# Hybrid decoder trunk: seven products for eight in the second matrix of each MLP's fourth quarter

## The chip, the cores and the metric

The kernel runs on one core of one Trainium2 chip. The metric is the device time of one execution in microseconds (us). The core has a matrix engine (TensorE, PE in the profile; PEld is its weight load), a vector engine (VectorE, DVE), a scalar engine with function tables (ScalarE, ACT), GpSimd (POOL) and SyncE (SP), which issues the transfers. Matrix products are accumulated in PSUM (8 banks of 512 float32 columns); all else lies in SBUF. Each engine works through its own queue in order, and waits on semaphores for the others.

## The reference

Two layers over 528 positions (16 learned meta tokens and 512 inputs) of width 1024, in float32:

```
layer 0: h = h + mixer(rms_norm(h))          sliding-window attention and Mamba-2, then w_out
         h = h + square(relu(rms_norm(h) @ w_up[0])) @ w_down[0]
layer 1: h = h + conformer(rms_norm(h))      pw1, sigmoid gate, causal convolution of 31 taps,
                                             layer norm, SiLU, pw2
         h = h + square(relu(rms_norm(h) @ w_up[1])) @ w_down[1]
out = h without the meta positions
```

`w_up` is 1024 x 4096 and `w_down` 4096 x 1024 in each layer; `pw1` is 1024 x 2048, `pw2` 1024 x 1024.

## The kernel before

**Layout.** Activations are held transposed: 128 channels on the partitions, positions along the row. The 528 positions are cut into stream A (272 positions, 256 after the meta tokens are dropped) and stream B (256). A product takes a 128x128 tile of weights as the loaded operand and one stream's columns as the moving one.

**Precision.** A float32 product is made from three in the type `float32r`. Each operand is split in a high part, a rounded copy, and a low part, the rest: hi x hi, hi x lo and lo x hi are accumulated in one bank (`products`, L456). Splitting a piece of weights costs a cast on ScalarE (`th_cast`, L410, tile `wh`) and a subtraction on VectorE or GpSimd (`th_low`, L423, tile `wl`). Activations are split likewise (`ah` and `al`, `nh` and `nl`).

**Stages.** An MLP goes in four quarters q of 1024 hidden channels. "up" makes eight hidden tiles: `ev_up` (L1325) does relu with the norm's factor `rb` (VectorE), the square (ScalarE), the copy `ah` (ScalarE) and the rest `al` (VectorE). "dn" multiplies them with the matching quarter of `w_down` into eight output tiles, and `ev_dn` (L1340) adds each to `h`. In the profile `up03A` is layer 0, quarter 3, stream A. With a positive `lead`, `dense` (L468) begins that many output tiles together, does the first `cut` of their inner tiles, and only then the rest: this covers the wait for the last inputs. After w_out the order is: layer 0 A q2, q3 (A q0, q1 are done earlier); pw1 of A, `pw1(0)`; layer 0 B q0 to q3; `pw1(1)` of B; `pw2(0)`; layer 1 A q0 to q3; `pw2(1)`; layer 1 B q0 to q3. The last quarter of a stream ends with `prep` (L1225), which makes the next norm's inputs, or with `fin` (L1604), which writes the output. In layer 1 both streams have 256 columns.

**The convolution.** `th_conv` (L1484) runs on VectorE in the background, 31 taps for each of 8 channel tiles of a stream, in PSUM, once pw1's evacuation has written the gated tiles `U`. `th_ln` (L1528) then makes the layer norm and SiLU and writes the split inputs of pw2, `KHr[0]` and `KLr[0]` for A and `AH[1]` for B. Ahead of `pw2(0)` and of `pw2(1)` the main thread waits for this thread (`pause("ln")`).

**Weights.** `expect` lists the pieces of all weights in the order of use; `th_load` brings them through SyncE into a pool of wide buffers (8 tiles, 512 KB) or narrow ones (4 tiles, 256 KB), with 3 and 4 buffers each for raw, high and low parts.

**What sets the order.** All instructions are written down by a list scheduler (`Sched`, L66) when the kernel is built. Threads offer one operation at a time; `step` (L177) takes the one that can start first by modelled times, ties going to the lower priority number (evacuations 0.5, casts, layer norm 1, convolution 3, products 5). An operation may have two ways, VectorE or GpSimd; `emit` (L121) takes the one that ends first. In this model VectorE operations with two inputs in SBUF and GpSimd operations exclude each other ("port"). For the low parts `bias` is added to VectorE's end: 600 ns, 3000 from pw1(0) on, 0 from pw2(1) on. On the chip only the order within each queue and the choice of engine remain.

## Time and profile before

| | |
|---|---|
| median of 3 runs | 1237.41 us (1237.12 to 1237.72) |
| profiled execution | 1237.84 us, of which the span from first to last instruction is 1236.1 us |
| mean granted TensorE clock | 0.994 |
| TensorE busy | 1219.7 us, 9939 matrix instructions |
| VectorE, ScalarE, GpSimd busy | 861.5, 683.4, 549.5 us |
| loaded from HBM | 190.62 MB |

A time of a stretch is written as from:to in microseconds from the span's start. In a group of instructions `out<-in` names what is written and read, then partitions x elements, the count, the busy time and the mean of one, and last the engine's idle time before them with what ended it. Matrix instructions overlap in the pipeline, so a mean of 285 ns doesn't mean that one starts every 285 ns.

### The profile page before, as it was taken

The page shows a single profiled execution, that of the slowest core. Times are in us where ns is not written, and L with a number is a line of the kernel's source. Part 1 is how long each engine was busy: PE and PEld are TensorE (multiplying, and loading weights), DVE is VectorE, ACT ScalarE, POOL GpSimd, SP SyncE. Part 2 cuts the span into 40 slices and gives each one's busy share as a digit, 9 for nine tenths or more (in the row PEclk, how much of TensorE's full clock was granted, in tenths as well). Part 3 has the DMA queues.
Part 4 walks back from the last instruction along what each step waited for, and adds up shares of the span by engine and source line. Part 5 has one row for each costly group of instructions (what it writes and reads, how often), then busy time and mean ns, then how long its engine had stood idle before and what let it go on. Part 6 is the DMA issues. An engine that isn't in the chain of part 4 may idle for free.

```text
span 1236.1 us, 25626 instructions
## 1 busy us (share of the span) xinstructions
PE 1219.7 (99%) x9939; PEld 1176.1 (95%) x9939; DVE 861.5 (70%) x1915; ACT 683.4 (55%) x1277; POOL 549.5 (44%) x339
## 2 busy tenths in 40 slices
PE   8999998999999999999999999999999999999998
PEld 7999887799898999999999999999999999999998
DVE  6745685787785675658989965589898626766664
ACT  6654235677475663654544568556345645644542
POOL 0112331354541111148888878888888781000000
PEclk8999999999999999999999999999999999999999
DMA  6323112344344765546555555565555566566562
GB/s 191 105 81 86 44 44 56 104 141 144 114 142 135 245 198 176 172 135 199 183 184 181 185 166 180 187 192 175 181 186 183 176 194 202 188 179 196 177 196 91
DMA packets 79961, 194.38 MB, mean 157 GB/s; under 512 B 8912, under 2 KB 16608, under 8 KB 79840
## 3 DMA queue, kind: packets, MB, share of 16 engines
q1 hardware_dynamic: 79840, 192.75, 50.2%
q8 instruction: 78, 1.28, 0.4%
q14 instruction: 43, 0.35, 0.1%
HBM read 190.62 MB, written 2.10 MB: 156 GB/s over the span
## 4 chain that ended last, share of the span: by engine, by line
PE 92%; DVE 3%; ACT 3%; issue 1%; DMA 1%; SPq 0%; DVEq 0%; ACTq 0%
PE in L308 11%; PE pw L308 9%; PE out L308 5%; PE dn00A L308 2%; PE up00A L308 2%; PE up01A L308 2%; PE up03A L308 2%; PE dn02A L308 2%; PE dn12A L308 2%; PE up03B L308 2%; PE dn13B L308 2%; PE dn12B L308 2%; PE dn11B L308 2%; PE dn10B L308 2%; PE dn11A L308 2%; PE dn03B L308 2%
## 5 line engine op out<-in xcount | busy, mean ns | idle before, releaser
L256 POOL TENSOR_TENSOR wl<-wr,wh 128x1024 fp32r<-128x1024 f32 (+1 forms) x292 | 519.2, 1798 | 432.1 <-ACT wh L280 315.3
L280 ACT CAST wh<-wr 128x512 fp32r<-128x512 f32 (+1 forms) x494 | 384.6, 801 | 287.7 <-PE in L308 35.1
L254 DVE TENSOR_TENSOR wl<-wr,wh 128x512 fp32r<-128x512 f32 (+1 forms) x202 | 189.3, 949 | 90.0 <-ACT wh L280 87.1
L261 DVE SCALAR_TENSOR_TENSOR conv<-U,vec,conv 128x256 f32<-128x256 f32 x464 | 211.3, 484 | 5.2
L308 PE MATMUL in<-xh,wh 128*128 128x272 f32 (+1 forms) x384 | 103.6, 296 | 1.4 <-ACT wh L280 1.2
L308 PE MATMUL in<-xl,wh 128*128 128x272 f32 (+1 forms) x384 | 100.8, 289 | 1.1 <-DVE xl L261 1.1
L308 PE MATMUL pw<-nh,wh 128*128 128x256 f32 (+1 forms) x320 | 80.3, 285 | 0.0
L308 PE MATMUL pw<-nl,wh 128*128 128x256 f32 (+1 forms) x320 | 80.1, 284 | 0.0
L308 PEld LDWEIGHTS in<-xh,wh 128*128 128x128 f32 x384 | 73.3, 191 | 6.9 <-issue 3.2
L308 PEld LDWEIGHTS in<-xl,wh 128*128 128x128 f32 x384 | 73.3, 191 | 2.3 <-DVE xl L261 2.0
L308 PE MATMUL in<-xh,wl 128*128 128x272 f32 (+1 forms) x384 | 66.9, 291 | 0.0
L308 PEld LDWEIGHTS pw<-nl,wh 128*128 128x128 f32 x320 | 60.3, 189 | 0.0
L308 PEld LDWEIGHTS pw<-nh,wh 128*128 128x128 f32 x320 | 60.2, 188 | 0.1
L308 PEld LDWEIGHTS in<-xh,wl 128*128 128x128 f32 x384 | 55.0, 192 | 1.6 <-issue 0.9
L308 PE MATMUL pw<-nh,wl 128*128 128x256 f32 (+1 forms) x320 | 48.4, 284 | 0.0
L276 ACT ACT_TABLE_LOAD x30 | 38.5, 1283 | 9.0 <-DMA hin<-in_h 4.6
L308 PEld LDWEIGHTS pw<-nh,wl 128*128 128x128 f32 x320 | 42.8, 188 | 0.0
L308 PE MATMUL out<-xh,wh 128*128 128x272 f32 (+1 forms) x128 | 33.0, 288 | 0.2 <-ACT acc L276 0.2
L308 PE MATMUL out<-xl,wh 128*128 128x272 f32 (+1 forms) x128 | 32.6, 285 | 0.0
L254 DVE TENSOR_TENSOR pw<-pw,rb 128x272 f32<-128x272 f32 (+1 forms) x32 | 14.1, 440 | 24.9 <-PE pw L308 24.9
L308 PEld LDWEIGHTS out<-xh,wh 128*128 128x128 f32 x128 | 24.1, 188 | 1.4 <-issue 0.8
L308 PEld LDWEIGHTS out<-xl,wh 128*128 128x128 f32 x128 | 24.1, 188 | 0.0
(597 smaller groups left out, 3642.5 us busy)
## 6 DMA issues: line engine op xcount, KB each, us to landing
wr<-in_w_up SPq DMA_DIRECT2D x84, 512.0 KB, 3.7
wr<-in_w_dn SPq DMA_DIRECT2D x84, 512.0 KB, 4.0
wr<-in_w_up SPq DMA_DIRECT2D x88, 256.0 KB, 4.3
wr<-in_w_dn SPq DMA_DIRECT2D x88, 256.0 KB, 4.3
wr<-in_w_p SPq DMA_DIRECT2D x36, 512.0 KB, 3.9
wr<-in_w_in SPq DMA_DIRECT2D x48, 256.0 KB, 2.9
wr<-in_w_out SPq DMA_DIRECT2D x36, 256.0 KB, 2.8
wr<-in_w_p SPq DMA_DIRECT2D x24, 256.0 KB, 5.2
```

Source lines behind the costliest of these rows:

```text
L254: ways = [("V", 1.04 * n + 145, lambda: nc.vector.tensor_tensor(o, a, b, op=op), sb(a) and sb(b))]
L256: ways.append(("G", 2.17 * n + 170, lambda: nc.gpsimd.tensor_tensor(o, a, b, op=op), True))
L261: lambda: nc.vector.scalar_tensor_tensor(o, a, s, b, op0=op0, op1=op1), sb(a) and sb(b))],
L276: return Op([("A", ns, lambda: nc.scalar.activation(o, a, f, **kw), False)], aps(o, accum), aps(a, scale, bias), table=TABLE.get(f, 0))
L280: return Op([("A", 0.836 * cols(o) + 192, lambda: nc.scalar.copy(o, a), False)], [o], [a])
L308: nc.tensor.matmul(o, lhsT=l, rhs=r, start=st, stop=sp)
```

## The change

The dn matrix of quarter 3 is done for both streams at once, in both layers. Two rows of weight tiles and two halves of the inner tiles make a 2x2 block matrix W, the halves of the hidden channels and the two streams a 2x2 block matrix (X for A, Y for B). Strassen's scheme (in Winograd's form) makes the product with seven block products in place of eight. It needs four sums of weight blocks per pair of rows (`th_sum`, tile `ws`, on VectorE or GpSimd) and four sums of activation blocks (`sums_of`), each split in high and low parts, and sums of the results: `ev` in `seven` and `add_part` or `fin_part`, which add to `h` in two steps. The sums of activations lie in the room of `U` and `Y`, the convolution's tiles, which are now taken for the time of the convolutions only.

For this, both streams' up of quarter 3 go together, tile by tile, in the order 0, 4, 1, 5, 2, 6, 3, 7, and the order of the stages changes. Layer 0: A's q2 is cut in two halves of four hidden tiles, one before and one after the joint q3; B's q0 to q2 follow pw1(0) as before. Layer 1: A q0 to q2 before pw2(1), B q0 to q2 after it, the joint q3 last. `late=False` lets B's q0 in layer 0 apply the norm's factor in up rather than in dn.

Two more edits act on the whole kernel. In `step`, while a thread of priority up to 0.5 offers an operation for VectorE that excludes GpSimd, other threads' GpSimd operations that would end after its start are held off. `row_norm` keeps one PSUM bank for both of its steps instead of two in turn.

```diff
         for th in self.threads:
             op = th[3]
             if op is None:
                 continue
...
+            t = min(self.start(op, w)[0] for w in ways)
             t = max(t, op.dep + op.late)
-            p = th[1]
-            p = p() if callable(p) else p
+            p = rank(th)
...
+    def expect_seven(pairs):
+
+
+        for one, two in pairs:
+            i = len(plan)
+            half = lambda j, x: (j, 4 * x)
+            plan.extend((("wp", one, 8, None), ("wp", two, 8, "raw"),
+                         ("wm", (ALU.add, half(i + 1, 0), half(i + 1, 1)), 4, "sum"),
+                         ("wm", (ALU.subtract, half(i, 0), half(i + 1, 0)), 4, "sum"),
+                         ("wm", (ALU.subtract, half(i + 2, 0), half(i, 0)), 4, "sum"),
+                         ("wm", (ALU.subtract, half(i, 1), half(i + 4, 0)), 4, "sum"),
+                         ("wm", half(i + 1, 1), 4, "half")))
+            uses.extend((4, 4, 2, 1, 2, 1, 1))
...
+            if plan[i][3] == "sum":
+                op, (a, x), (b, y) = plan[i][1]
+                yield lambda: a in raws and b in raws
+                t = yield take(wm, [128, 4, 128], F32, "raw", 4, "ws")
+                o = TT(t, raws[a][:, x:x + 4], raws[b][:, y:y + 4], op, True)
+                o.ways[0] += (bias[0] / 2,)
+                yield o
+                raws[i] = t
+                used_raw(a, b)
...
-        yield BM(*((p[:, i:i + 1], a[:, blk(c)[0] - b0:blk(c)[0] - b0 + 128], ones[:, 0:1], True, True)
+        yield BM(*((p[:, 496 + i:497 + i], a[:, blk(c)[0] - b0:blk(c)[0] - b0 + 128], ones[:, 0:1], True, True)
...
-        yield TS(v, p[:, :nb], 1.0 / D, eps, ALU.mult, ALU.add)
-        drop(p)
+        yield TS(v, p[:, 496:496 + nb], 1.0 / D, eps, ALU.mult, ALU.add)
...
-        p = yield bank("bg", "st" + key)
...
+            if last:
+                raw[s, j] = yield take(pool7[0], [128, 272], F32, "sq", 8)
+                r = raw[s, j][:, :w]
+                yield ACT(r, u, AF.Square)
+                drop(p)
+                sums.add((s, j))
+                if s == 0 or j >= 4:
+                    yield CP(ah[:, j, :w], r)
+                    yield TT(al[:, j, :w], r, ah[:, j, :w].bitcast(F32), ALU.subtract)
+                    up[i].add(j)
+                return
...
+        if last:
+            summed = [set() for _ in range(4)]
+            flat.clear()
+            for t, x in (("U", TAPS - 1 + T), ("Y", T)):
+                flat.append((yield take(pool7[0], [128, 8 * x], F32R, t, 1)))
+            for k in range(4):
+                spawn(sums_of(k, streams[0][4], sums, raw, up, summed), 1, name + "sum")
+        yield from dense(name, nts, 8, [t[1:5] for t in streams], ev_up, lead, cut, [has(t[6]) for t in streams])
+        name = name.replace("up", "dn")
+        if last:
+            yield from seven(name, streams, up, summed, last)
+        else:
+            yield from dense(name, range(8), m, [(t[7], t[8], 0, t[4]) for t in streams], ev_dn,
+                             dlead, dcut, [(lambda k, u=u: k in u) for u in up])
...
+    SEVEN = (0, 4, 1, 5, 2, 6, 3, 7)
...
+    def sums_of(k, w, there, raw, up, summed):
+        yield lambda: {(0, k), (1, k)} <= there
+        x1, y1 = raw[0, k], raw[1, k]
+        yield lambda: k in up[0]
+        yield TT(x1[:, :256], y1[:, :256], x1[:, :256], ALU.subtract, True)
+        yield lambda: (1, k + 4) in there
+        y2 = raw[1, k + 4]
+        yield TT(y1[:, :256], y2[:, :256], y1[:, :256], ALU.subtract, True)
+        yield lambda: k + 4 in up[1]
+        yield TT(y2[:, :256], y2[:, :256], x1[:, :256], ALU.subtract, True)
+        if w > 256:
+            yield VCP(y2[:, 256:w], x1[:, 256:w])
+        yield lambda: k + 4 in up[0]
+        x2 = raw[0, k + 4]
+        yield TT(x2[:, :w], y2[:, :w], x2[:, :w], ALU.subtract, True)
+        for i, t in ((1, x1), (3, y1), (2, y2), (4, x2)):
+            n = w if i in (2, 4) else 256
+            hi, lo = slot(i, 0, k, n), slot(i, 1, k, n)
+            yield CP(hi, t[:, :n])
+            yield TT(lo, t[:, :n], hi.bitcast(F32), ALU.subtract, True)
+            drop(t)
+            summed[i - 1].add(k)
+
+    def seven(name, streams, up, summed, part):
...
+        def sbank():
+            t = pmm(name)()
+            return t if t is not None else bank("at", name)()
+
+        def product(p, hi, lo, x, first, last_, ks=range(4)):
+            xh_, xl_, when, n = ops[x]
+            for k in ks:
+                yield lambda: when(k)
+                yield MM([(p[:, :n], hi[:, k], xh_(k), first and k == 0, False),
+                          (p[:, :n], hi[:, k], xl_(k), False, False)])
+            for k in ks:
+                yield MM([(p[:, :n], lo[:, k], xh_(k), False, last_ and k == 3)])
...
+            yield lambda: "M1" in at
+            yield CP(m1[:, :w], b[0][:, :w])
+            at.add("m1")
+            yield lambda: "M6" in at
+            yield TT(u[:, :w], m1[:, :w], b[3][:, :w], ALU.add)
+            drop(b[3])
+            yield TT(u7[:, :256], u[:, :256], b[2][:, 0:256], ALU.add)
+            drop(b[2])
+            if w > 256:
+                yield VCP(u7[:, 256:w], u[:, 256:w])
+            yield TT(u[:, :256], u[:, :256], b[1][:, 0:256], ALU.add)
...
+            def p11():
+                yield from part(n, ca, w, m1[:, :w], lambda: b[0][:, :w], ALU.add, lambda: "M2" in at)
+                end(m1, b[0])
+
+            def p22():
+                yield from part(n + 1, cb, 256, u7[:, :256], lambda: b[1][:, 0:256], ALU.add, lambda: "M5" in at)
+                at.add("22")
+                last_of(u7)
+
+            def p12():
+                yield from part(n, cb, 256, u[:, :256], lambda: b[1][:, 256:512], ALU.add, lambda: "M3" in at)
+                yield lambda: "22" in at
+                end(u, b[1])
+
+            def p21():
+                yield from part(n + 1, ca, w, u7[:, :w], lambda: b[4][:, :w], ALU.subtract, lambda: "M4" in at)
+                end(b[4])
+                last_of(u7)
+            for g in (p22(), p11(), p12(), p21()):
+                spawn(g, 0.5, name + "ev")
+        for n in range(0, 8, 2):
+            b, at = [], set()
+            b.append((yield sbank))
+            x = yield from piece()
+            spawn(ev(n, b, at), 0.5, name + "ev")
+            terms = [("X1", "M1", x)]
+            for t, m in ((1, "M5"), (3, "M7"), (2, "M6")):
+                terms.append((f"T{t}", m, None))
+
+            for ks in ((0, 1, 2), (3,)) if n == 0 else (range(4),):
+                for i, (t, m, pc) in enumerate(terms):
+                    if pc is None:
+                        b.append((yield sbank))
+                        pc = yield from piece()
+                        terms[i] = (t, m, pc)
+                    yield from product(b[i], pc[0], pc[1], t, True, True, ks)
+                    if ks[-1] == 3:
+                        if i:
+                            done_with(*pc[:2])
+                        at.add(m)
+            yield lambda: "m1" in at
+            yield from product(b[0], x[0][:, 4:], x[1][:, 4:], "X2", True, True)
+            done_with(*x[:2])
+            at.add("M2")
+            pc = yield from piece()
+            yield from product(b[1][:, 256:], pc[0], pc[1], "Y2", True, True)
+            done_with(*pc[:2])
+            at.add("M3")
+            b.append((yield sbank))
+            pc = yield from piece()
+            yield from product(b[4], pc[0], pc[1], "T4", True, True)
+            done_with(*pc[:2])
+            at.add("M4")
+        yield lambda: len(summed[3]) == 4
+        drop(*flat)
...
+    def add_part(n, c0, w, x, y, op, when):
+        hn = h[0][:, n, c0:c0 + w]
+        yield TT(hn, hn, x, ALU.add, True)
+        yield when
+        yield TT(hn, hn, y(), op)
...
-        yield from mlp(0, 2, [(*A[0], *AH[0], add_h)], 0, 0, 2)
-        yield from mlp(0, 3, [(*A[0], *AH[0], prc[0])], 0, 0, 2)
+        yield from mlp(0, 2, [(*A[0], *AH[0], add_h)], 0, 0, 2, 3, inner=(16, 4))
+        wide[0] = 2
+        bias[0] = 600.0
+        pool7.append(lp)
+        yield from mlp(0, 3, [(*A[0], *AH[0], None), (*A[1], *AH[1], None)], last=add_part)
+        wide[0] = 1
+        yield from mlp(0, 2, [(*A[0], *AH[0], prc[0])], 0, 0, 2, 3, inner=(20, 4))
+        U = yield take(lp, [128, 8, TAPS - 1 + T], F32, "U", 1)
+        Y = yield take(lp, [128, 8, T], F32, "Y", 1)
+        yield Op([("G", 400, lambda: nc.gpsimd.memset(U[:, :, 0:TAPS - 1], 0.0), True)], [U[:, :, 0:TAPS - 1]], [])
...
-        for q in range(NQ):
-            yield from mlp(0, q, [(*A[1], *AH[1], add_h if q < NQ - 1 else prc[1])], 0, 0, 2)
+        for q in range(3):
+            yield from mlp(0, q, [(*A[1], *AH[1], add_h if q < 2 else prc[1])], 0, 0, 2, late=False)
...
-        def fin(n, c0, w, p):
+        def fin_part(n, c0, w, x, y, op, when):
+            hn = h[0][:, n, c0:c0 + w]
+            yield TT(hn, hn, x, ALU.add, True)
+            yield when
             o = yield take(lt[0], [128, 272], F32, "ut", 2)
-            yield TT(o[:, :w], p[:, :w], h[0][:, n, c0:c0 + w], ALU.add)
-            drop(p)
+            yield TT(o[:, :w], hn, y(), op)
             yield DMA(out[n * 128:n * 128 + 128, c0 - NM:c0 - NM + w], o[:, :w], 128)
             drop(o)
-        for q in range(4):
-            yield from mlp(1, q, [(*F[0], *AH[0], add_h if q < 3 else fin)], 2 if q == 0 else 0, 6, 2)
+        for q in range(3):
+            yield from mlp(1, q, [(*F[0], *AH[0], add_h)], 2 if q == 0 else 0, 6, 2)
         yield from pause("ln")
+        drop(U, Y)
         bias[0] = 0.0
         yield from pw2(1, *AH[1], prf[1])
-        for q in range(4):
-            yield from mlp(1, q, [(*F[1], *AH[1], add_h if q < 3 else fin)], 2 if q == 0 else 0, 6, 2)
+        for q in range(3):
+            yield from mlp(1, q, [(*F[1], *AH[1], add_h)], 2 if q == 0 else 0, 6, 2)
+        wide[0] = 2
+        bias[0] = 600.0
+        yield from mlp(1, 3, [(*F[0], *AH[0], None), (*F[1], *AH[1], None)], last=fin_part)
```

178 lines of the change are left out of this document (122 added, 56 removed).

## The prediction

> **What bounds the kernel now.** I read the page first, then the busy times by stretch.
>
> ```profile
> span 1236.1 us, 25626 instructions
> PE 1219.7 (99%) x9939; PEld 1176.1 (95%) x9939; DVE 861.5 (70%) x1915; ACT 683.4 (55%) x1277; POOL 549.5 (44%) x339
> PE 92%; DVE 3%; ACT 3%; issue 1%; DMA 1%; SPq 0%; DVEq 0%; ACTq 0%
> ...
> core 0: us, PE busy (x) PEld busy (x) DVE busy (x) ACT busy (x) POOL busy (x), PEclk, DMA share, GB/s
> 460.40:484.50 24.10, 24.10 (x194) 24.10 (x194) 13.48 (x17) 9.16 (x13) 3.63 (x2) 1.00 0.57 176
> 653.40:676.10 22.70, 22.70 (x195) 22.70 (x193) 20.76 (x49) 8.99 (x13) 19.36 (x11) 1.00 0.63 191
> 769.60:838.00 68.40, 68.40 (x581) 68.28 (x580) 49.11 (x120) 39.22 (x66) 58.72 (x31) 1.00 0.60 188
> 838.00:1026.00 188.00, 187.64 (x1575) 187.05 (x1574) 136.09 (x332) 102.53 (x179) 155.84 (x81) 1.00 0.59 185
> ```
>
> TensorE is busy 99% of the span and is 92% of the chain that ended last. One half quarter of an MLP is 8x8x3 = 192 products. With 256 columns it takes 22.70 us (653.4 to 676.1), 118.2 ns a product; with 272 columns 24.10 us, 125.5 ns. In these stretches TensorE never rests, so a product taken away is 118 ns won, as long as nothing else becomes late. The reader should also see VectorE in the third stretch: 20.76 of 22.70 us. It is there because the depthwise convolution (248 instructions per stream) runs in the background, and that work has a due time of its own:
>
> ```profile
> L308 PE MATMUL dn03B<-ah,wl x64: 276/280/284, 747.9 to 769.6; 128*128 128x256 f32 x64
> L308 PE MATMUL pw<-ah,wh x64: 278/280/355, 1026.3 to 1048.1; 128*128 128x256 f32 x64
> L261 DVE SCALAR_TENSOR_TENSOR conv<-U,vec,conv 128x256 f32<-128x256 f32 x232 | 105.7, 483 | 2.4
> L261 DVE SCALAR_TENSOR_TENSOR Y<-U,vec,conv x16: 471/474/478, 636.2 to 956.0; 128x256 f32<-128x256 f32 x16
> 795.12 1.39 DVE L261 SCALAR_TENSOR_TENSOR conv<-U,vec,conv 128x256 f32<-128x256 f32 x3
> 977.91 0.42 DVE L254 TENSOR_TENSOR al<-stln,ah 128x256 fp32r<-128x256 f32 x1 [0.83 <-ACT ah L280]
> 988.40 0.42 DVE L254 TENSOR_TENSOR al<-lnq,ah 128x256 fp32r<-128x256 f32 x1 [0.91 <-ACT ah L280]
> 988.50:1026.00 37.50, 37.50 (x319) 37.50 (x318) 8.26 (x20) 18.25 (x30) 32.93 (x17) 1.00 0.65 205
> ```
>
> Stream B's pw1 begins at 769.6, when dn03B ends. The convolution of stream B goes from 795.1 to 956.5, its layer norm delivers the eight input tiles of pw2(1) from 978.3 to 988.8, and pw2(1) takes them at 1026.2. The slack is 37.4 us, less than the 45.4 us of one full quarter. The change moves such a quarter (layer 1, q3 of stream A) from before pw2(1) to the end. This is the number on which my forecast turns.
>
> **The change part by part.**
>
> *Products.* Each layer's dn of q3 for both streams has 2x192 = 384 products before and 4 pairs x 7 x 12 = 336 after. The columns saved are always 256 wide, so 2x48x118.2 ns = -11.35 us. The merged up of q3 has the same products as before.
>
> *The wait at pw2(1).* After pw1(1)'s start TensorE has pw1(1) and pw2(0) (68.4 us), then four quarters before and three after. 256.6 us (769.6 to 1026.2) less 45.4 us leaves 211.2. The convolution chain gives its last tile at 988.8 - 769.6 = 219.2 us after the same start. It can't shrink much: from 795 to 956 VectorE does 232 taps of 483 ns and the evacuations at the same rate as before, since these belong to the same stages. TensorE starts pw2(1) with the tiles that are there and takes 0.236 us for a tile's two products, so it would need the eighth at 211.2 + 7x0.236 = 212.9. It stands 219.3 - 212.9 = 6.4 us. With less competition at the end (TensorE waits, so no evacuations and fewer casts) it could be 3 us less; with the first stream's layer norm now running into pw1(1) it could be more (a rival below). I take 6.4.
>
> *The split q2.* In layer 0 stream A's q2 is cut in two halves of 4 tiles round the merged q3. The cover at each up-to-dn step shrinks: the two leading dn tiles do 3 k each, not 6, so the wait for the last tile is hidden by 2x3x3x125.5 ns = 2.26 us.
>
> ```profile
> L308 PE MATMUL up02A<-nh,wl x64: 285/287/293, 435.9 to 460.3; 128*128 128x272 f32 x64
> L254 DVE TENSOR_TENSOR al<-up02A,ah x8: 426/431/435, 446.5 to 463.6; 128x272 fp32r<-128x272 f32 x8
> L308 PE MATMUL up13A<-nh,wl x64: 276/280/284, 981.8 to 1003.4; 128*128 128x256 f32 x64
> L254 DVE TENSOR_TENSOR al<-up13A,ah x8: 417/424/425, 985.6 to 1005.5; 128x256 fp32r<-128x256 f32 x8
> ```
>
> In up02A the last `al` ends 3.7 us after the last product starts, in up13A 2.5 us. So each of the two steps costs 0.2 to 1.4 us; I take 0.75, together +1.5. The second half's dn feeds the next norm at 1.5 us a tile in place of 3: ScalarE then has a cast of a 128x512 piece (0.617 us) and three instructions of about 0.42 us in that time, a little over; the casts are done ahead, so I count nothing and keep 1 us for the range.
>
> *Making the seven's operands.* Per pair of row tiles, weights need one 128x1024 split, five 128x512 splits and four 128x512 sums, and evacuation one copy, three sums and eight additions.
>
> ```profile
> L256 POOL TENSOR_TENSOR wl<-wr,wh 128x1024 fp32r<-128x1024 f32 x126 | 301.8, 2406 | 90.9 <-ACT wh L280 85.6 <-PE dn12A L308 2.9 <-PE dn10A L308 2.4
> L256 POOL TENSOR_TENSOR wl<-wr,wh 128x512 fp32r<-128x512 f32 x166 | 219.6, 1336 | 341.2 <-ACT wh L280 229.6 <-DVE wl L254 37.6 <-PE out L308 29.0
> L254 DVE TENSOR_TENSOR wl<-wr,wh 128x1024 fp32r<-128x1024 f32 x41 | 50.2, 1224 | 35.8 <-ACT wh L280 35.7
> L254 DVE TENSOR_TENSOR wl<-wr,wh 128x512 fp32r<-128x512 f32 x26 | 17.1, 683 | 0.0
> L254 DVE TENSOR_TENSOR h<-dn12B,h 128x256 f32<-128x256 f32 x8 | 3.4, 420 | 2.0 <-PE dn12B L308 2.0
> L280 ACT CAST wh<-wr 128x1024 fp32r<-128x1024 f32 x210 | 220.5, 1051 | 214.1 <-PE pw L308 19.5 <-PE dn10A L308 15.4 <-PE dn02A L308 14.3
> L280 ACT CAST wh<-wr 128x512 fp32r<-128x512 f32 x284 | 169.6, 617 | 73.6 <-PE in L308 35.1 <-issue 13.0 <-PE dn00A L308 6.3
> L254 DVE TENSOR_TENSOR rs_rln<-rs_rln,rs_tln 128x2 f32<-128x2 f32 x1 | 2.3, 2311 | 0.0
> L254 DVE TENSOR_TENSOR rs_tln<-rs_tln,rs_vln 128x2 f32<-128x2 f32 x1 | 0.2, 160 | 0.0
> ```
>
> On VectorE alone (the rows of the last stage, where GpSimd is idle) that is 1.22 + 9x0.68 = 7.4 us, and 11x0.42 = 4.6 us for evacuation: 12.0 us per pair against 7x12x118.2 ns = 9.9 us of TensorE. GpSimd must take a part, at 1.34 us for a 512 piece. The two 128x2 rows show the price: the same kind of operation took 2311 ns beside a running GpSimd split and 160 ns without, so the two engines get at SBUF in turn. GpSimd can still work while VectorE reads PSUM, 7x0.42 = 2.9 us per pair, two 512 pieces, which leaves VectorE 10.7 us. The four pairs thus need about 43 us against 40, but the first pair's weights and the second's first piece (some 9 us) are made during the 45 us of up. So the sum comes out even. Bounds: below, 0; above, 0.8 us for each of the three later pairs, 2.4 us per layer. I take 0.4 per layer, near the lower end because of the head start, +0.8. The sums of activations have 4.3 us of cover (36 products of k 0 to 2) at the start; the last tile's chain (three additions, a copy and a subtraction of 0.4 us behind the usual 2.5 us) is about 4.5 us and enters with the last of these: 0. ScalarE has 1.05 + 5x0.617 + 0.4 = 4.5 us per pair: hidden.
>
> *Loads.* Two streams share q3's weights: 16 fewer pieces of 512 KB per layer (and eight 256 KB pieces more where q2 is cut). DMA engines are about 60% busy in the rows above; nothing on the path.
>
> *The end.*
>
> ```profile
> 1232.87 0.42 DVE L254 TENSOR_TENSOR ut<-dn13B,h 128x256 f32<-128x256 f32 x1 [2.41 <-PE dn13B L308]
> out_t<-ut SPq DMA_DIRECT2D x16, 128.0 KB, 2.4
> ```
>
> Four outputs now end within 4.3 us (three products of 1.42 us after M6) through two `ut` buffers, each held 2.8 us (0.42 + 2.4). With M6's end as 0, the outputs are written at about 2.4 and 2.8, and their buffers free at 4.9 and 5.3; the last sum starts at 5.3, not at 4.5: +0.8.
>
> *The hold-off, the one-bank row norm.* Both act before 434 us too. The most they can win there is the one long wait of TensorE, 4.36 us with 2.4 us of lower clock behind it (rows below); the most they can lose I bound by one more such wait. TensorE is else busy there, so I take 0. `late=False` spares eight 0.43 us multiplications in the first convolution, off the path.
>
> Sum: -11.35 + 6.4 + 1.5 + 0.8 + 0.8 = -1.85 us. The profiled execution took 1237.84 us (span 1236.1), 0.03% over the median of 1237.41; against the median 1235.6.
>
> **The rivals.**
>
> *A: the whole gain comes (about 1230).* If stream B's layer norm ends early enough, -11.35 + 3.1 = -8.2, so 1229.2; at the 3 us of relief above 1232.6. For it: the last 8 us of the layer norm share ScalarE with casts that a waiting TensorE no longer asks for. Against it: the 240 taps ahead of it keep their pace.
>
> *B: the first layer norm delays the second convolution (slower).* The first convolution and its layer norm end 180 and 220 us after pw1(0) starts at 533.2; with a quarter fewer between, pw1(1) now starts after about 187 us, so this layer norm runs inside pw1(1).
>
> ```profile
> L308 PEld LDWEIGHTS pw<-nh,wh x320: 186/188/193, 533.2 to 837.5; 128*128 128x128 f32 x160
> 636.00:713.00 77.00, 77.00 (x647) 76.79 (x647) 70.24 (x170) 38.49 (x63) 64.52 (x33) 1.00 0.58 178
> 713.00:753.20 40.20, 40.20 (x336) 39.99 (x335) 23.59 (x59) 28.81 (x58) 29.57 (x17) 1.00 0.51 158
> L276 ACT ACT_TABLE_LOAD x30 | 38.5, 1283 | 9.0 <-DMA hin<-in_h 4.6
> ```
>
> Its Silu and pw1's Sigmoid need different tables at 1.28 us a load. If five sigmoids fall among the Silus, ten loads are 12.8 us of ScalarE, and the gates `U`, on which the convolution waits, come later by some 6 us. Each of these microseconds is paid again at pw2(1): -1.85 + 6 = +4.2, 1241.6. It turns slower at 4.3 us of delay (0.2%). Against it: the scheduler runs three Silus in a row, so fewer loads.
>
> *C: the clock falls in the wait.*
>
> ```profile
> 213.42 0.47 PE L315 MATMUL att_b<-cm,pm 128*128 128x128 f32 x1 [4.36 <-DVE pm L254]
> 211.00:213.00 2.00, 0.00 (x0) 0.00 (x0) 0.93 (x7) 2.00 (x9) 0.00 (x0) 0.61 0.00 0
> 213.00:215.00 2.00, 1.58 (x8) 1.48 (x9) 1.49 (x5) 1.61 (x6) 0.00 (x0) 0.50 0.00 0
> 215.00:217.00 2.00, 2.00 (x6) 0.78 (x5) 0.00 (x0) 1.72 (x3) 0.00 (x0) 0.50 0.64 199
> 217.00:219.00 2.00, 2.00 (x10) 0.83 (x8) 0.32 (x1) 1.68 (x3) 0.00 (x0) 0.68 0.28 71
> ```
>
> After 4.36 us without work the granted clock stood at 0.50 until about 218: 1.58x0.5 + 2x0.5 + 2x0.32 = 2.4 us lost on top of the wait. If the 6.4 us at pw2(1) does the same, -1.85 + 2.4 = +0.6, 1238.0. Against it: TensorE isn't quite idle there, since tiles come one by one. The Trainium skill ("TensorE: Matmul & The Clock Gate", Part 1) states that the array falls to half rate after an idle window of about 3.4 us and needs as long a busy one to come back; the rows above agree (6 us from about 212 to 218), and by that rule this rival holds.
>
> **How the numbers follow.** About 0.2% (2.5 us) is what a measurement of this kernel tells from no change: faster below 1234.9, slower above 1239.9. Forecast (a wait of a few us at pw2(1), 1233 to 1237.5): 0.42, of which a good half lies within 0.2%. A (1228 to 1233): 0.27. B: 0.16. C: 0.15, mostly within 0.2%. Faster 0.42x0.43 + 0.27 = 0.45, slower 0.14 + 0.05 = 0.19, same 0.36. The range takes A's lower part and B's first half: 1229 to 1241. Time 1235.6.
>
> **What would show it.** TensorE with 9843 products, 40 us for layer 1's seven-product stage and 41 for layer 0's; one gap of 5 to 9 us in total at pw2(1)'s first `ah`, released by VectorE's `al` or ScalarE's `ah`; waits of about a microsecond at the two halves of dn02A. I am wrong if there is no such gap (A), if the second convolution starts later than 27 us after pw1(1) (B), if the clock shows 0.5 behind the gap (C), or if the seven-product stages take more than 43 us.

## The result and the profile after

The changed kernel took 1246.89 us (median; 1245.93 to 1248.80) beside 1237.26 us for the kernel before: a ratio of 1.0082 (95% interval 1.0064 to 1.0099). It is 9.6 us slower; forecast were 1235.6 us and a range up to 1241. The profiled execution took 1245.93 us with a span of 1244.1 us. From the page of the changed kernel, the span, the busy time of each engine and the engines of the chain that ended last:

```profile
span 1244.1 us, 25517 instructions
PE 1214.9 (98%) x9843; PEld 1165.6 (94%) x9843; DVE 925.0 (74%) x2069; ACT 683.6 (55%) x1310; POOL 510.9 (41%) x331
PE 89%; DVE 4%; issue 2%; ACT 2%; POOL 1%; DMA 0%; SPq 0%; DVEq 0%; POOLq 0%; ACTq 0%
```

The 96 products are gone (9939 to 9843), VectorE has 63 us more work, and TensorE's share of the chain fell from 92% to 89%: it waits. Where, the busy time by stretch tells. Columns: the stretch and its length, then busy us (and instructions) of PE, PEld, DVE, ACT and POOL, the granted clock, the DMA share, GB/s. The kernel before, cut where the same stages begin and end (stream A's q2 in layer 0; pw1(1) with pw2(0); pw2(1)):

```profile
434.90:484.60 49.70, 49.41 (x395) 49.19 (x394) 32.32 (x52) 26.42 (x46) 6.54 (x5) 1.00 0.58 183
...
769.70:838.80 69.10, 69.10 (x587) 68.98 (x586) 49.59 (x121) 39.92 (x68) 59.42 (x31) 1.00 0.61 190
1026.30:1049.20 22.90, 22.90 (x194) 22.75 (x193) 17.17 (x30) 13.92 (x29) 0.00 (x0) 1.00 0.66 195
```

The changed kernel: q2's first half, dn03AB (seven products), q2's second half, pw1(1) with pw2(0), pw2(1), dn13AB (seven products):

```profile
432.90:458.90 26.00, 25.57 (x202) 25.13 (x201) 18.69 (x36) 13.89 (x30) 7.00 (x5) 1.00 0.53 164
...
505.70:549.20 43.50, 41.96 (x338) 41.34 (x337) 36.45 (x71) 18.67 (x33) 13.31 (x12) 1.00 0.32 97
549.20:577.00 27.80, 24.87 (x194) 24.26 (x193) 20.55 (x40) 16.86 (x41) 8.30 (x7) 1.00 0.47 154
...
767.70:841.90 74.20, 71.06 (x590) 69.84 (x590) 56.43 (x144) 55.73 (x93) 57.18 (x31) 1.00 0.52 163
...
984.60:1012.20 27.60, 26.20 (x194) 24.59 (x193) 18.78 (x36) 17.69 (x38) 2.93 (x3) 0.94 0.49 143
...
1196.40:1239.80 43.40, 41.40 (x338) 40.02 (x336) 36.88 (x70) 15.99 (x30) 15.76 (x11) 1.00 0.29 87
```

Without a wait dn13AB would take 336 x 118.2 ns = 39.7 us, and dn03AB, where four of seven products have 272 columns, 4 x (48 x 125.5 + 36 x 118.2) ns = 41.1 us. So, in us:

| term | forecast | profile |
|---|---|---|
| products | -11.35 | -11.35 |
| the two stages by seven (43.5 - 41.1, 43.4 - 39.7) | +0.8 | +6.1 |
| q2 in halves (26.0 + 27.8 - 49.7) | +1.5 | +4.1 |
| pw1(1) with pw2(0) (74.2 - 69.1) | 0 | +5.1 |
| pw2(1) (27.6 - 22.9) | +6.4 | +4.7 |
| from TensorE's last product to the end (3.2 to 4.4) | +0.8 | +1.2 |
| start, to stream A's q2 (434.9 to 432.9) | 0 | -2.0 |
| sum (span: +8.0) | -1.85 | +7.9 |

The row of the start is no gain of the change: own_bank (below) has the same instructions up to there and begins stream A's q2 at 435.6 us.

**pw1(1).** ScalarE's groups in this stage, first of the kernel before (769.7 to 838.8), then of the changed one (767.7 to 841.9):

```profile
L276 ACT ACT_TABLE_LOAD x2 | 2.6, 1283 | 0.0
```

```profile
L285 ACT ACT_TABLE_LOAD x10 | 12.8, 1283 | 0.2
```

Stream A's layer norm now runs in this stage; its Silu and the gates' Sigmoid take the table from each other, eight loads more (in the whole run 36, not 30). ScalarE's casts of weights come late with them, and TensorE waits up to 0.8 us at a time, as here:

```profile
785.20 0.39 PE L317 MATMUL pw<-nh,wh 128*128 128x256 f32 x1 [0.80 <-ACT wh L289]
```

**pw2(1).** The timeline, VectorE and then TensorE, with the wait and its releaser in brackets at the end of a line:

```profile
797.25 2.84 DVE L270 SCALAR_TENSOR_TENSOR conv<-U,vec,conv 128x256 f32<-128x256 f32 x6
...
989.56 0.42 DVE L263 TENSOR_TENSOR al<-lnq,ah 128x256 fp32r<-128x256 f32 x1 [0.42 <-ACT ah L289]
986.39 0.38 PE L317 MATMUL pw<-ah,wh 128*128 128x256 f32 x1 [0.43 <-ACT ah L289]
...
987.90 0.38 PE L317 MATMUL pw<-al,wh 128*128 128x256 f32 x1 [0.35 <-DVE al L263]
```

Two stretches of 3.4 us by engine, at the same place:

```profile
985.70:989.10 3.40, 2.28 (x8) 1.21 (x8) 2.60 (x7) 2.82 (x8) 1.83 (x2) 1.00 0.88 267
989.10:992.50 3.40, 3.37 (x14) 3.04 (x14) 0.54 (x3) 1.45 (x3) 0.00 (x0) 0.50 0.11 42
```

The taps begin 29.6 us after pw1(1)'s start (25.4 before), and the layer norm's last tile is ready 222.3 us after it (219.2 before). TensorE comes at 216.9, takes the tiles one by one as they arrive, and then has half the clock for 3.4 us: 14 products where 28.8 would fit, 1.7 of the 4.7 us. This half clock is not in every execution: in own_bank both TensorE and the last tile come at the same times after pw1(1) (216.9 and 222.3), the clock stays at 1.00, and pw2(1) takes 26.6 us in place of 27.6.

**The stages by seven and the end.** In dn13AB, VectorE's third sum into `u`, then TensorE in the middle of product M3; and the last sums before the outputs:

```profile
1205.51 0.42 DVE L263 TENSOR_TENSOR sq<-sq,dn13AB 128x256 f32<-128x256 f32 x1 [0.57 <-PE dn13AB L317]
...
1205.98 0.50 PE L317 MATMUL dn13AB<-ah,wl 128*128 128x256 f32 x2 [0.51 <-DVE sq L263]
...
1240.63 0.91 DVE L263 TENSOR_TENSOR ut<-h,dn13AB 128x256 f32<-128x256 f32 x2 [1.51 <-DMA out_t<-ut]
```

VectorE waits for TensorE, and TensorE for VectorE: M3 is accumulated in columns 256 to 511 of the bank whose columns 0 to 255 hold M5, which the sum reads. In q2's second half the steps are a bank given back late and a cast that comes late:

```profile
553.53 0.36 PE L317 MATMUL up02A<-nh,wh 128*128 128x272 f32 x1 [1.14 <-DVE h L263]
575.43 0.40 PE L317 MATMUL dn02A<-ah,wh 128*128 128x272 f32 x1 [1.70 <-ACT wh L289]
```

### The profile page after: what moved, and what is told of

The parts are those of the page before. It is cut to its first block, busy times and chain, and to the rows that moved or that the text cites. A ratio compares the mean times of both kernels' runs of the same rounds, so it can differ in the third digit from the quotient of the medians.

```text
span 1244.1 us, 25517 instructions
## 1 busy us (share of the span) xinstructions
PE 1214.9 (98%) x9843; PEld 1165.6 (94%) x9843; DVE 925.0 (74%) x2069; ACT 683.6 (55%) x1310; POOL 510.9 (41%) x331
## 3 DMA queue, kind: packets, MB, share of 16 engines
q1 hardware_dynamic: 74512, 175.97, 45.7%
## 4 chain that ended last, share of the span: by engine, by line
PE 89%; DVE 4%; issue 2%; ACT 2%; POOL 1%; DMA 0%; SPq 0%; DVEq 0%; POOLq 0%; ACTq 0%
PE in L317 11%; PE pw L317 8%; PE out L317 5%; PE up03AB L317 4%; PE up13AB L317 4%; PE dn03AB L317 3%; PE dn13AB L317 2%; PE up00A L317 2%; PE up01A L317 2%; PE dn00A L317 2%; PE dn01A L317 2%; PE dn02B L317 2%; PE dn12A L317 2%; PE dn11A L317 2%; PE dn10A L317 2%
## 5 line engine op out<-in xcount | busy, mean ns | idle before, releaser
L265 POOL TENSOR_TENSOR wl<-wr,wh 128x1024 fp32r<-128x1024 f32 (+1 forms) x256 | 447.5, 1771 | 424.3 <-ACT wh L289 357.0
L289 ACT CAST wh<-wr 128x512 fp32r<-128x512 f32 (+1 forms) x457 | 346.4, 783 | 257.1 <-issue 28.6
L263 DVE TENSOR_TENSOR wl<-wr,wh 128x512 fp32r<-128x512 f32 (+1 forms) x201 | 180.7, 908 | 76.5 <-ACT wh L289 70.6
L265 POOL TENSOR_TENSOR sq<-sq,sq 128x256 f32<-128x256 f32 x3 | 3.0, 998 | 188.4 <-DVE al L263 188.4
L285 ACT ACT_TABLE_LOAD x36 | 46.2, 1283 | 4.3 <-DMA hin<-in_h 3.7
L317 PE MATMUL up03AB<-nl,wh 128*128 128x256 f32 (+1 forms) x128 | 32.0, 285 | 0.0
L317 PE MATMUL up03AB<-nh,wh 128*128 128x256 f32 (+1 forms) x128 | 32.0, 284 | 0.0
```

Source lines behind the costliest of these rows:

```text
L263: ways = [("V", 1.04 * n + 145, lambda: nc.vector.tensor_tensor(o, a, b, op=op), sb(a) and sb(b))]
L265: ways.append(("G", 2.17 * n + 170, lambda: nc.gpsimd.tensor_tensor(o, a, b, op=op), True))
L285: return Op([("A", ns, lambda: nc.scalar.activation(o, a, f, **kw), False)], aps(o, accum), aps(a, scale, bias), table=TABLE.get(f, 0))
L289: return Op([("A", 0.836 * cols(o) + 192, lambda: nc.scalar.copy(o, a), False)], [o], [a])
L317: nc.tensor.matmul(o, lhsT=l, rhs=r, start=st, stop=sp)
```

## The experiments

The ratios are to the kernel before, with 95% intervals; the changed kernel stands at 1.0082.

### The stages by seven: one bank, or VectorE

**own_bank**: M3 gets a bank of its own.

```
-            yield from product(b[1][:, 256:], pc[0], pc[1], "Y2", True, True)
+            b.append((yield sbank))
+            yield from product(b[4], pc[0], pc[1], "Y2", True, True)
...
-            yield from product(b[4], pc[0], pc[1], "T4", True, True)
+            yield from product(b[5], pc[0], pc[1], "T4", True, True)
```

> Product M3 gets a bank of its own instead of the second half of M5's bank; nothing else changes. Theory (shared bank): M3's products stopped in the middle for VectorE's sum over the first half of that bank, and the sum for them, some 0.7 to 1.2 us for each of the eight pairs. Then the two stages by seven products fall from 43.8 and 43.4 us to 40.5 to 41.5, and the time from 1246.9 to about 1242. Rival (operands late): what stops TensorE in these stages is the making of the operands, and the stop only moves to another product; the time stays within 1 us of 1246.9.

Measured: 1243.91 us, 1.0052 (1.0037 to 1.0067). The two stages, layer 0 and layer 1:

```profile
508.30:552.70 44.40, 42.07 (x339) 41.48 (x338) 39.71 (x73) 18.18 (x32) 13.99 (x12) 1.00 0.31 97
1197.60:1238.70 41.10, 40.62 (x338) 39.85 (x336) 37.65 (x70) 15.98 (x30) 15.79 (x11) 1.00 0.30 93
```

In layer 1 the shared bank was 2.3 of the 3.7 us lost. In layer 0 nothing came back: TensorE now waits at the start of a pair for a bank. So the theory holds for one stage of the two.

**own_bank_wide**: the same, with `wide[0] = 3` in place of 2 in both joint stages.

> M3 in a bank of its own, and in both joint stages one more bank may be taken from the background's three. Theory (with a bank of its own layer 0 lacked a bank: three waits of 0.4, 1.3 and 1.5 us for the sums to give one back): dn03AB falls from 44.3 to 41.5, dn13AB stays at 41.1; 1241 to 1242. Rival (VectorE makes the sums too late in layer 0 whatever banks there are): layer 0's stage stays above 43 us and the time at 1243.9.

Measured: 1245.54 us, 1.0060 (1.0045 to 1.0075). Layer 0's stage takes 44.4 us as before, with TensorE's waits at the start of a pair still there:

```profile
530.59 0.36 PE L317 MATMUL dn03AB<-ah,wh 128*128 128x272 f32 x1 [1.00 <-DVE h L263]
542.36 0.36 PE L317 MATMUL dn03AB<-ah,wh 128*128 128x272 f32 x1 [1.22 <-DVE h L263]
```

But this does not decide for the rival. The edit did not reach layer 0: there the two programs are the same, instruction for instruction, and every tile of dn03AB has the PSUM bank that it had in own_bank; they differ only from the second pair of dn13AB on. The scheduler took no bank that only the wider limit allows. What the trace does show is why VectorE's sums, which give the bank back, are late at these two places. Ahead of the first wait, VectorE and then GpSimd:

```profile
526.47 3.65 DVE L263 TENSOR_TENSOR h<-h,sq 128x272 f32<-128x272 f32 x3
...
526.87 1.50 POOL L265 TENSOR_TENSOR wl<-ws,wh 128x512 fp32r<-128x512 f32 x1
528.33 1.49 POOL L265 TENSOR_TENSOR ws<-wr,wr 128x512 f32<-128x512 f32 x1
```

Three additions to `h` took 3.65 us while GpSimd made operands; in the same stage one took 0.43 us when GpSimd stood still. Ahead of the second wait it is 3.66 us. That is some 2.4 us more each time, and TensorE waits 1.0 and 1.2 us. No run here took GpSimd away from these places, so that it is the cause of the waits is likely and not shown; whether another bank would cover them is open too (bank 4 is not used in this stage).

**m4_first**: M4, which has a bank of its own, ahead of M3, so that M3 starts 1.5 us later; `expect_seven` lists the two pieces of weight in the new order.

> Product M4, which has a bank of its own, is made ahead of M3, which shares a bank with M5; no bank is added. Theory (shared bank): when M3 starts, 1.5 us later than now, VectorE has read M5's half, so neither stops; the stages by seven products fall from 43.5 and 43.3 us by some 2 us each, and no bank is missing in layer 0, as it was with a bank more: 1242 to 1244. Rival (VectorE gives the banks back too late in layer 0, whatever the order): layer 0's stage stays at 43.5 us and only layer 1 gains: 1244.5 to 1246.

Measured: 1253.10 us, 1.0126 (1.0111 to 1.0141), 6 us worse than the change, against theory and rival. The stages grow to 47.2 and 46.2 us (in the second the profile has 3.4 us of half clock). In dn13AB:

```profile
1211.42 0.74 DVE L263 TENSOR_TENSOR ut<-h,dn13AB 128x256 f32<-128x256 f32 x2
...
1211.88 0.38 PE L317 MATMUL dn13AB<-ah,wh 128*128 128x256 f32 x1 [2.03 <-DVE ut L263]
```

My expectation overlooked that VectorE reads M5's half twice: once for `u`, and once more for the output of row n+1, column half B. M3 now meets the second read, behind four additions of `h` on VectorE's queue. This fits the shared bank as the cause, and a later start does not cure it. That a separate bank cures it in layer 1 is shown; whether two halves of one bank could be used at once, no run here tried.

### The order of stages

**order_only**: both streams' q3 together and q2 in halves, but eight products.

```
-        yield from mlp(0, 3, [(*A[0], *AH[0], None), (*A[1], *AH[1], None)], last=add_part)
+        yield from mlp(0, 3, [(*A[0], *AH[0], add_h), (*A[1], *AH[1], add_h)], 0, 0, 2)
```

> The order of stages of the changed kernel (the fourth quarters of both streams together, the third quarter of layer 0 in two halves), but all products by eight: no sums, no shared banks. Theory (the order costs what the trace shows in the second pw1, at the second pw2 and in the halves; the stages by seven products cost 6.4 us of their own and the end 1): 1246.9 + 11.35 - 7.4 = about 1251. Rival (the sums load VectorE and GpSimd and make the rest late): 1247 or less.

Measured: 1251.82 us, 1.0123 (1.0104 to 1.0142). pw1(1) with pw2(0) takes 74.2 us and pw2(1) 27.7 us, as in the changed kernel, and the joint dn stages 46.8 and 45.7 us without a wait. This run has the hold-off and the one-bank row norm too; beside hold_off_alone (below, 1239.39 us), which has them in the old order, the order costs about 12 us by itself. The seven products give back 4.9 of their 11.35 us.

**layer1_only**: layer 0 as before, layer 1 as changed.

> Layer 0 as in the kernel before (each stream's four quarters together, eight products), layer 1 as in the changed kernel. Theory (one chain from pw1 to the end of the second layer norm sets when the second pw2 can run): the second pw1 runs clean again (69.1 us with pw2 beside it, not 74.3) and the convolution starts 25.5 us after it, but TensorE reaches the second pw2 that much sooner too, so the wait there grows from 4.7 to 6 to 8 us; with 3.7 in the stage by seven products and 1.0 at the end, less 5.7 of products: 1242 to 1244. Rival (the losses of the two places only add up, and that at pw2 stays at 4.7 or falls with the earlier convolution): 1238 to 1241.

Measured: 1241.33 us, 1.0041 (1.0027 to 1.0055), between the rival's 1241 and the theory's 1242. pw1(1) is back at 69.1 us, pw2(1) takes 28.3 us: the loss there did grow, from 4.7 to 5.4 us, less than I had it, and 1.3 us of it is half clock (18 products in 3.4 us). Layer 0's part of the change therefore makes the kernel 5 us slower in all, though it saves 5.7 us of products.

### The chain from pw1(1) to pw2(1)

**half_taps**: in the changed kernel 16 of the convolution's 31 taps.

```
-                for j in range(TAPS):
+                for j in range(0, TAPS, 2):
```

> The convolution uses 16 of its 31 taps (every second one is left out of the computation); TensorE's work is the same. Theory (the convolution's chain): both convolutions end some 70 us sooner, so the first layer norm lies ahead of the second pw1, and the second finds its tiles ready. Then the 5.2 us lost in the second pw1, the 4.7 at the second pw2 and some of the rest vanish: 1236 to 1238. The losses in the two stages by seven products (6.4 us) and their end stay. Rival (shared engines in general, VectorE and GpSimd too full everywhere): the stages by seven products gain as much, and the time falls to 1232 or under.

**before_half_taps**: the same cut in the kernel before.

> The kernel before, with 16 of the convolution's 31 taps (every second one left out of the computation). Theory (the convolution is hidden in the kernel before and bounds the changed one alone): 1236 to 1238, no change, while the same cut took 10 us off the changed kernel. Rival (it costs time in both): 1233 or less.

Measured: 1236.60 us, 0.9997 (0.9987 to 1.0007), and 1238.47 us, 1.0004 (0.9992 to 1.0016). Half a convolution takes 10 us off the changed kernel and nothing off the one before. With it pw2(1) takes 22.8 us, the clock stays at 1.00, and the first layer norm lies ahead of pw1(1); dn03AB and dn13AB stay at 43.6 and 43.2 us. This is the plainest finding of the study: the change turned a background chain into one that TensorE waits for. It shows also what is left without that chain: the stages by seven still lose 6.0 us, q2 in halves 4.1 and the end 1.2, which is all of the 11.35 us of products.

**silu_by_sigmoid**: stream A's layer norm without the Silu table.

```
-                yield ACT(u, yk(k), AF.Silu, bias=V("lnb", k))
+                if s == 0:
+                    yield ACT(u, yk(k), AF.Sigmoid, bias=V("lnb", k))
+                    yield STT(u, yk(k), V("lnb", k), u, ALU.add, ALU.mult)
+                else:
+                    yield ACT(u, yk(k), AF.Silu, bias=V("lnb", k))
```

> In the first layer norm alone Silu is made as a Sigmoid on ScalarE and one more VectorE product, so that it uses the table of the gates of the second pw1; the result is the same. Theory (table changes): with no table loads between the two, the second pw1 and the pw2 beside it take 70 us, not 74.3, the convolution starts 26 us after pw1 instead of 29.6, the wait at the second pw2 falls from 4.7 us to about 1, and with it the stretch of half clock goes; time about 1239. Rival (load of VectorE): the eight more VectorE operations of about 0.6 us and the layer norm's own sums are what makes it late; the time stays at 1246 to 1249.

Measured: 1247.41 us, 1.0080 (1.0065 to 1.0095): no gain. Its three stretches from pw1(1) on:

```profile
767.00:836.40 69.40, 69.40 (x589) 69.40 (x589) 58.66 (x149) 44.92 (x86) 58.40 (x31) 1.00 0.58 179
836.40:983.70 147.30, 144.11 (x1187) 142.88 (x1185) 125.39 (x298) 75.17 (x130) 117.44 (x62) 0.99 0.56 175
983.70:1012.50 28.80, 27.75 (x193) 25.59 (x194) 19.98 (x40) 18.24 (x40) 1.76 (x2) 0.88 0.43 136
```

The tables did cost pw1(1) its 5 us: two loads are left and the stage runs clean. But pw2(1) ends 245.5 us after pw1(1) starts, with the Silu 244.5, and the rival's forecast holds. With eight more operations on VectorE the taps begin 3.4 us sooner (26.2 us after pw1(1)), yet the convolution ends 0.6 us later (191.5, not 190.9) and the last tile comes 1.0 us later (223.3). Of the time that pw1(1) gave back, 2.9 us go in up10A. There one operation on the row statistics of the next norm holds VectorE for 2.2 us, and TensorE waits for the `al` behind it:

```profile
844.13 2.23 DVE L277 TENSOR_SCALAR rs_tfn<-rs_tfn 128x2 f32<-128x2 f32 x1
846.73 0.38 PE L317 MATMUL up10A<-nh,wh 128*128 128x256 f32 x1 [1.23 <-DVE al L263]
```

The clock is also at half for 3.4 us there, and in pw2(1) for 6.8 us, not 3.4. So the stall that was mended ahead of the chain's end gained nothing; that all of it came back through this one chain is not shown.

**relu_on_act**: eight VectorE operations of 0.43 us beside the second convolution go to ScalarE.

```
-                yield TS(u, u, 0.0, None, ALU.max)
+                yield ACT(u, u, AF.Relu) if layer and not s else TS(u, u, 0.0, None, ALU.max)
```

> The eight ReLUs of stream A's first quarter in layer 1, which VectorE makes beside the second convolution (0.43 us each), go to ScalarE; nothing else changes. Theory (VectorE's load sets when the second layer norm ends): 3.4 us less on VectorE in this stretch, the layer norm ends about 3 us sooner after pw1, and the 4.7 us lost at the second pw2 fall to 1 or 2, without the half clock: 1243. Rival (the chain is late because it starts late, 29.6 us after pw1): no change beyond 1 us.

Measured: 1247.52 us, 1.0087 (1.0069 to 1.0106): no gain, as the rival had it, but not by its reason. The convolution ended 186.1 us after pw1(1), 4.8 us sooner; the layer norm's last tile came only 1.1 us sooner. Between lie operations on 128x2 row statistics. Two of VectorE's groups in the changed kernel, then two of them in relu_on_act, and there GpSimd's timeline:

```profile
L277 DVE TENSOR_SCALAR rs_tln<-rs_tln 128x2 f32<-128x2 f32 x1 | 1.2, 1224 | 0.0
L263 DVE TENSOR_TENSOR rs_tln<-rs_tln,rs_vln 128x2 f32<-128x2 f32 x1 | 0.9, 903 | 0.0
```

```profile
L263 DVE TENSOR_TENSOR rs_tln<-rs_tln,rs_vln 128x2 f32<-128x2 f32 x1 | 1.4, 1369 | 0.0
L263 DVE TENSOR_TENSOR rs_rln<-rs_rln,rs_tln 128x2 f32<-128x2 f32 x1 | 0.5, 534 | 0.0
```

```profile
971.88 11.98 POOL L265 TENSOR_TENSOR wl<-wr,wh 128x1024 fp32r<-128x1024 f32 x6 [2.67 <-PE dn12A L317]
```

Operations that take 0.16 us alone took up to 1.8 us here, with GpSimd at work without a break; from the first of them to the first use 12.4 us went by (8.8 in the changed kernel). The stretched operations are only 0.9 of the 3.6 us of difference. Most of the rest is the order in VectorE's queue, where additions to `h` stand between them and wait for TensorE's dn12A (3.4 us, in the changed kernel 1.4):

```profile
977.82 0.42 DVE L263 TENSOR_TENSOR h<-dn12A,h 128x256 f32<-128x256 f32 x1 [1.14 <-PE dn12A L317]
980.66 0.42 DVE L263 TENSOR_TENSOR h<-dn12A,h 128x256 f32<-128x256 f32 x1 [1.62 <-PE dn12A L317]
```

The change's hold-off does not help: the layer norm's thread has rank 1, and only ranks to 0.5 hold off.

**hold_off_rank1**: `URGENT = 1.0` in place of 0.5.

> The hold-off is extended: threads of rank 1 or less (the layer norms, the sums, the casts) count as urgent, not only those of 0.5 or less. Theory (the second layer norm's row statistics are stretched by GpSimd: its six VectorE operations on 128x2 took 0.2 to 1.2 us each and 8.8 us from the first to the first use, with 0.16 us as the shortest): they take 0.2 us each, the layer norm ends 4 to 5 us sooner, and the 4.7 us lost at the second pw2 fall under 2, without the half clock: about 1243. Rival (the time of these operations is in the semaphores between engines, or the low parts of the weights are then late): 1246 to 1250, with new waits for GpSimd's wl.

Measured: 1259.94 us, 1.0181 (1.0164 to 1.0198). Three of the four stretched operations do fall to 0.16 us, but the kernel's start is hit: stream A's q2 begins at 447.9 us, not 432.9, and the clock stands at half for 31 us of the time from 210 to 272 us (3.4 in the changed kernel). And the last tile still comes 222.0 us after pw1(1), since from the first use of the statistics to that tile 12.7 us pass now, 11.3 in the changed kernel; why was not separated. The experiment mixed two places, so I narrowed it.

**late_hold_relu**: relu_on_act, and the hold-off for rank 1 only from the second convolution on.

> The changed kernel with two edits: stream A's first ReLUs in layer 1 on ScalarE, and the hold-off extended to rank 1 only from the second convolution on, so that the first 770 us are as in the changed kernel. Theory (VectorE's load and GpSimd's stretching of the row statistics are together what makes the second layer norm late): it ends 214 us after pw1, as when all was mended, not 222, before TensorE comes at 217; nothing is lost at the second pw2 and the clock stays: 4 to 5 us less than 1246.9, 1242 to 1243. Rival (the two do not add up, or the low parts of the weights come late instead): 1245 or more.

Measured: 1243.67 us, 1.0042 (1.0027 to 1.0056), and pw2(1) takes 25.2 us at a clock of 1.00. Together the two edits do what neither relu_on_act nor hold_off_rank1 did, though less than expected in the chain (last tile at 219.8, not 214); the half clock is gone in this profile. The late hold-off by itself was not run.

### What the hold-off is worth

**no_hold_off**: the changed kernel without the rule.

> The rule by which an urgent VectorE operation holds off GpSimd is undone (the bound set so that no thread is urgent); all else is as in the changed kernel. Theory (the losses are in the order of stages): the rule moves the time by at most 2 us either way, 1245 to 1249. Rival (the rule starves GpSimd, whose low parts of the weights come late in the second pw1): 1240 to 1243, with the steps released by GpSimd's low parts gone.

**hold_off_alone**: both layers by eight in the old order, with the hold-off and the one-bank row norm.

> Both layers' quarters as in the kernel before, all products by eight; of the change only the hold-off, the one-bank row norm and the first convolution's unmultiplied quarter stay. Theory (these are worth little): within 2 us of the kernel before, 1236 to 1239, since the start to the third quarter of layer 0 took 434.9 us before and 432.9 to 435.6 in the changed order where the clock did not fall. Rival (the hold-off gains the 3 us by which the run without it began later): 1234 or less.

Measured: 1249.04 us, 1.0091 (1.0074 to 1.0108), and 1239.39 us, 1.0013 (1.0003 to 1.0023). For the changed kernel the intervals with and without the rule overlap, so no effect is shown; with the row norm it costs 1.7 us in the old order. Without the rule pw2(1) runs clean (22.7 us), but dn10A takes 31.1 us in place of 24.5, with one long wait:

```profile
887.79 0.42 PE L317 MATMUL dn10A<-ah,wh 128*128 128x256 f32 x1 [4.44 <-DVE h L263]
```

### Can the seven products pay?

**all_mended** and **layer1_mended** put the edits together (own_bank, relu_on_act, hold_off_rank1, and the last sum made in `h` and sent from there; the first also `wide[0] = 3` and q2 split 2 + 6).

```
-            o = yield take(lt[0], [128, 272], F32, "ut", 2)
-            yield TT(o[:, :w], hn, y(), op)
+            yield TT(hn, hn, y(), op)
```

> Everything found so far together: M3's own bank with one bank more, the third quarter of layer 0 in halves of 2 and 6 tiles in place of 4 and 4, the ReLUs of stream A's first quarter on ScalarE, the hold-off for rank 1, and the last sum made in place of h and sent from there. Theory (the losses are those named: 6.4 in the stages by seven, 4.7 at the second pw2, 3.3 in the second half, 1.0 at the end): 5, 4, 2 and 1 us come back: 1234 to 1236, under the kernel before. Rival (one chain and one VectorE are full; what is won in one place is waited for in the next): 1239 or more.

> Layer 0 as before; layer 1 by seven products with M3's own bank, the ReLUs on ScalarE, the hold-off for rank 1, and the last sum in place. Theory: 5.7 us of products come back but for 1.3 in the stage by seven and 1 to 3 at the second pw2: 1233 to 1235.5. Rival (the wait at the second pw2 stays at 5.5 us, since TensorE comes there 45 us sooner than before): 1238.

Measured: 1251.67 us, 1.0113 (1.0090 to 1.0137), and 1246.30 us, 1.0069 (1.0054 to 1.0084): both worse than expected, because of the start that the hold-off for rank 1 lengthens. From stream A's q2 on they took 801.7 and 797.7 us, the kernel before 801.2, the changed one 811.2. pw2(1) was clean in both.

**layer1_late** and **both_late**: the same with the hold-off for rank 1 only from the second convolution on; both_late also with silu_by_sigmoid. **no_seven_late** is layer1_late's ReLU and late hold-off without any stage by seven.

```
+        URGENT[0] = 1.0
         spawn(th_conv(1), 3, "conv")
```

> Layer 0 as before; layer 1 by seven products with M3's own bank, the ReLUs on ScalarE, the last sum in place, and the hold-off for rank 1 from the second convolution on. Theory: from the third quarter of layer 0 on as in the run with layer 1 mended (797.7 us against 801.2 before), and the start as in the kernel before: 1233 to 1235. Rival (what precedes the second convolution gets slower too): 1238 or more.

> Both layers by seven products with all edits: M3's own bank with one more, the third quarter of layer 0 in halves of 2 and 6 tiles, the ReLUs on ScalarE, the last sum in place, the hold-off for rank 1 from the second convolution on, and Silu by Sigmoid in the first layer norm. Theory (the losses in the second pw1, 6.6 us when all was mended, are the table's): from the third quarter on 801.7 - 6 = 796 us: 1231 to 1234. Rival (Silu by Sigmoid puts 3.8 us on VectorE ahead of the second convolution and the wait comes back at the second pw2): 1236 to 1239.

> As hold_off_alone, and with the ReLUs on ScalarE and the hold-off for rank 1 from the second convolution on, as in layer1_late; no stage by seven products. Theory (nothing waits at the second pw2 here, so these edits gain nothing without the shorter stage): as hold_off_alone within 1 us, so that layer1_late's gain is that of the seven products. Rival (they gain by themselves): 1235 or less, and the seven products are worth nothing.

Measured: 1234.89 us, 0.9970 (0.9957 to 0.9982); 1235.15 us, 0.9970 (0.9960 to 0.9981); 1239.20 us, 1.0017 (1.0008 to 1.0026). Both are 0.3% faster than the kernel before, and the edits without seven products are not: no_seven_late is where hold_off_alone is. layer1_late from pw1(1) on (pw1(1) with pw2(0), stream A's q0 to q2, pw2(1), and last dn13AB):

```profile
769.70:838.80 69.10, 69.10 (x586) 68.98 (x585) 48.97 (x120) 39.47 (x68) 57.68 (x31) 1.00 0.59 183
838.80:980.30 141.50, 141.50 (x1187) 141.09 (x1186) 121.60 (x298) 80.47 (x146) 113.05 (x60) 1.00 0.58 178
980.30:1003.10 22.80, 22.80 (x195) 22.76 (x193) 16.36 (x30) 15.16 (x32) 4.78 (x3) 1.00 0.60 185
...
1187.20:1229.40 42.20, 40.95 (x338) 39.98 (x336) 38.09 (x73) 15.86 (x30) 12.23 (x10) 1.00 0.30 94
```

The layer norm's last tile comes 212.8 us after pw1(1), TensorE at 210.6: no wait at pw2(1). From stream A's q2 on layer1_late takes 799.0 us, no_seven_late 802.9: 3.9 of the 5.7 us of layer 1's products are kept. Their medians differ by 4.3 us. In layer 0 the seven products bring nothing even with all edits: both_late is no faster, and its dn03AB took 45.9 us.

## Why the prediction was wrong

*Products*: right. 9843 products, and 118 ns each where TensorE does not wait.

*The wait at pw2(1)* (6.4 us): the mechanism was right, and that the size came near (4.7) is in part luck. I let the chain run as before (219.2; the sum writes 219.3) and TensorE come at 211.2; in fact the chain was delayed by 3.1 us (222.3) and TensorE by 5.7 us (216.9), nearly all of it in pw1(1), and 1.7 of the 4.7 us are half clock. Without the half clock, in own_bank, the loss is 3.7 us. In layer1_only, where pw1(1) is clean, TensorE comes at 211.2 as in the sum and the last tile at 217.4; the loss is 5.4 us, 1.3 of them half clock.

*The first layer norm delays the second convolution* was rival B, at a chance of 0.16. It happened: 10 table loads, taps 29.6 us after pw1(1) (my bound was 27). I doubted it because Silus would run three in a row. I priced it only as a delay of the gates; it also made the casts late, and TensorE lost 5.1 us inside pw1(1) itself, which my sum put at nothing: this is the first step that failed. silu_by_sigmoid shows that this cost and the later waits are not independent terms: without the ten loads about the same time is lost further on. So what I should have added up is the whole stretch from pw1(1) to pw2(1), not its stages.

*The clock falls* was rival C, and it happened too in this execution: half the clock for 3.4 us, 1.7 us lost (priced at 2.4). My argument against it, that tiles come one by one and TensorE is never quite idle, does not hold in general: 8 products in 3.4 us did not keep the clock here, while the 15 and 14 of own_bank did.

*Making the seven's operands* (+0.8 us, bounds 0 to 2.4 per layer): the second step that failed, and the largest, with 6.1 us. I weighed VectorE's and GpSimd's throughput and left out that M3 shares a bank with M5. own_bank: 2.3 of layer 1's 3.7 us are that bank. The diff showed it (`b[1][:, 256:]`), and the Trainium skill says it in "PSUM — Partial Sum Buffer", section "Terms": two engines at one bank at once, TensorE writing and VectorE reading, is a collision error. No run here shows that error; the trace shows the two kept apart: M3 goes on 0.05 us after VectorE's sum ends (1205.51 + 0.42 to 1205.98). In layer 0 the shared bank is not what is missing: with it out of the way 3.3 us are still lost, above my bound of 2.4, and TensorE waits 2.2 us for VectorE's sums. My bound took the additions to `h` at 0.42 us each and let GpSimd work while VectorE reads PSUM; own_bank_wide's trace has them at up to 1.5 us, beside GpSimd.

*The split q2* (+1.5 us): 4.1, the third step. The two up-to-dn steps cost less than I said, about 0.3 us each in place of 0.75; most of the rest is a wait for a bank given back late after the joint stage (1.1 us) and one for the late cast (1.7 us). The latter I had seen, "a little over", and counted at nothing.

*The end* (+0.8): +1.2, by the mechanism named, `ut` held by its transfer for 1.5 us of waiting.

*Loads*: nothing, as said. *The hold-off, the one-bank row norm* (0, bounds -6.8 to +4.4): +1.7 us in hold_off_alone.

The sum was thus short by 5.1 (pw1(1)), 5.3 (seven) and 2.6 us (q2); the rows of pw2(1) and of the start took 3.7 us off again. *A*, the whole gain, comes in half the kernel only, and only after the chain is relieved.
